# Block kernel on one core: step 10's maximum in attention is issued behind step 9's low half

## The chip, the cores and the metric

The kernel is one program on one core of a Trainium2 chip. The metric is the device time of one execution in microseconds (us), as the median of several runs. All engines of the core run their own instruction streams and wait for each other by semaphores: TensorE (PE, with its weight loads as PEld), VectorE (DVE), ScalarE (ACT), GpSimd (POOL) and SyncE (SP, which issues transfers).

## The reference

One layer of a hybrid block on 512 latent tokens and 256 context tokens, width 2048. One projection of the normed and modulated tokens feeds grouped-query attention (12 query heads of 128, 4 key heads) and a Fourier mixing branch, both gated; the branches are merged by sigmoid gates and projected out. The part that the change touches is the softmax:

```
s = jnp.einsum('bqhgd,bkhd->bhgqk', qi, k, preferred_element_type=jnp.float32)
w = jax.nn.softmax(s, axis=-1).astype(v.dtype)
return jnp.einsum('bhgqk,bkhd->bqhgd', w, v)
```

There are 768 keys: the 512 latent tokens and the 256 context tokens. All products are kept at full float32 precision: each operand is split into a high and a low half, and a product is three matmuls.

## The kernel before

Attention is a loop over i = 0 to 47, twelve heads by four blocks of 128 queries (4 * NH steps), with three more rounds for the tail. In this text "step 10" is i = 10, the eleventh. A step has these parts, which stand in different rounds of the loop:

- `scores(i)`: six matmuls make the 128x768 scores, as 512 and 256 columns in three matmuls each; the DVE takes the negated maximum (TENSOR_REDUCE, L1494), and the ACT the exponential with its row sum (L1496). Below these are the scores, the maximum and the exponential of step i.
- `turn(i)`, one round later: six transposes on PE (L1512) turn the 128x768 probabilities; `split_from` then makes their high half on the ACT (L179, `pth`) and their low half on the DVE (L180, `ptl`). The high and low half of two steps fill one pair of tiles.
- `divide(i)`: the reciprocal of the row sum on the DVE (L1505) and a scaling of the head's gate on the ACT (L1506).
- `values(half)`, for two steps together: eighteen matmuls of 256 columns on PE that read `pth` and `ptl`, two transposes (L1527), then a copy (L1537) and a product (L1538).

Beside this run the filler (`fill`: matmuls of the Fourier branch's projection, with weights `whi` and `wlo` and 512 columns each, for which the DVE multiplies results at L1460), the turning of the next head's queries (L1359) and of the next key group's keys (L1352), sums of weights on POOL, and gate products (L1332). At the end of the loop the first matmuls of the next stage, `a_group(0)`, take the filler's place.

Where the data lies matters for the order. One PSUM tile `banks` of eight banks of 512 columns holds everything. Scores take columns 0 to 767, 768 to 1535 and 1536 to 2303 in turn (`wide[0]` to `wide[2]`), so two neighbours share bank 1; the turned probabilities lie at 2304 to 3071 (`wide[3]`), and share bank 4 with the third. A matmul into a shared bank waits until the other tenant has been read. So step 13's second piece waits for step 11's exponential, the scores of the third place for the low half of a turn, and so on.

The order of the instructions on each engine is not that of the loop. A scheduler lays all engines' streams out from the recorded work; `tc.issue_after(x)` keeps an instruction behind x. Each engine then works through its stream in order, and waits where an operand isn't there. So a change of one place in the order can shift all that follows it in the stage.

Of the kernel before, what the change touches and what calls it, by code (L numbers as in the profile page):

```python
# [27 lines left out]
NKEY = T + C  # L28
# [61 lines left out]
CHUNKS = (0, 2, 1, 3)  # L90
BRANCH_A, BRANCH_B = 10, (6, 7)
A_CHUNKS = ((0, 2), (1, 3))
SUM_AT = (10, 13, 16, 19, 25, 28)
CHAIN_FROM = {BRANCH_A + 1: 3, 8: 2, 9: 2}
HALVED = (8, BRANCH_A + 1)
# [26 lines left out]
def block_kernel(ctx, tc, xT, ctx_rows, ctx_toks, x, c_row, w_ss, w_gate, vecs, qkg, rope, dft_c, dft_s,  # L122
# [55 lines left out]
    def split_from(src, hi, lo):  # L178
        first = nc.scalar.activation(hi, src, ACT.Copy)  # L179
        return first, nc.vector.tensor_tensor(lo, src, hi.bitcast(F32), op=ALU.subtract)  # L180
# [149 lines left out]
    def give(*ts):  # L330
        free.extend(home.pop(id(t))[0] for t in ts)

    def mm3(o, ah, al, bh, bl, start, stop, cont=False):

        nc.tensor.matmul(o, ah, bh, start=start, stop=False, skip_group_check=cont)  # L335
        nc.tensor.matmul(o, ah, bl, start=False, stop=False, skip_group_check=cont)  # L336
        nc.tensor.matmul(o, al, bh, start=False, stop=stop, skip_group_check=cont)  # L337
# [1145 lines left out]
    def scores(i):  # L1483
        h, t = divmod(i, 4)
        kh, kl = kv[h // GQ][:2]
        s = slice(t * P, (t + 1) * P)
        qh, ql = qs[h][:, 0, s], qs[h][:, 1, s]
        sc = next_wide()

        m = 512 if sc is not wide[1] else 256  # L1490
        for a, b in ((0, m), (m, NKEY)):
            mm3(sc[:, a:b], qh, ql, kh[:, a:b], kl[:, a:b], True, True)
        mx = stats[:, 4 * (i % 4) : 4 * (i % 4) + 4]
        maxima[0] = nc.vector.tensor_reduce(mx[:, 0:1], sc[:, :NKEY], axis=AX.X, op=ALU.max, negate=True)  # L1494
        probs[i] = take((NKEY,))
        maxima[1] = nc.scalar.activation(probs[i], sc[:, :NKEY], ACT.Exp, bias=mx[:, 0:1], accum_out=mx[:, 1:2])  # L1496
        if t == 3:
            give(qs.pop(h))

    def divide(i):  # L1500

# [6 lines left out]
    def turn(i):  # L1508
        p = probs.pop(i)
        tp = wide[3]  # L1510
        for k in range(KT):
            nc.tensor.transpose(tp[:, k * P : (k + 1) * P], p[:, k * P : (k + 1) * P], ident)  # L1512
        if i % 2 == 0:
            pts[i // 2] = [atp.tile([P, KT, 256], F32R, tag=n, bufs=2, name=uid(n)) for n in ("pth", "ptl")]
        c = slice((i % 2) * P, (i % 2) * P + P)
        split_from(tp[:, :NKEY].rearrange("p (k q) -> p k q", k=KT), *(w[:, :, c] for w in pts[i // 2]))
        give(p)

    def values(half):
        h, second = divmod(half, 2)  # L1520
# [126 lines left out]
    for i in range(NSTEP + 3):  # L1647
        h, t = divmod(i, 4)
        if i < NSTEP:
            if t == 2 and h + 2 < NH:  # L1650
                load_head(h + 2)
            if i % 12 == 10 and i // 12 + 1 < NKV:
                get_keys(i // 12 + 1)
            scores(i)
        want = min(3 + 61 * (i + 1) // NSTEP, 64) + (i == NSTEP - 1)
        if want > filled:
            fill(1)
            filled += 1
        if i % 2 == 0 and i >= 4:
            values((i - 4) // 2)  # L1660
        if 1 <= i <= NSTEP:
            turn(i - 1)
            divide(i - 1)
        if t == 1 and h + 1 < NH:
            turn_queries(h + 1, b1())
        if want > filled:
            fill(want - filled)
            filled = want
        n = next((n for n, at in enumerate(SUM_AT) if at <= i < at + 3), None)
        if n is not None:  # L1670
            step = i - SUM_AT[n]
            if step == 0:
                weight_sum(n)
            else:
                summed[-1][step]()
            if step == 2:
                give(summed.pop()[0])
        if i == 3:
            with tc.issue_after(maxima[0].ins), tc.issue_after(maxima[1].ins):
                e = take((1024,))  # L1680
                silu_of_row(1, e)
                give(e)
        if i == 33:
            for p in more_raw:
                raw_pools.remove(p)
                retired.append(p)
                if not any(r is p for a in ahead for r, _ in a.raws):
                    free.append(p[0::2])
        if i in GATE_STEPS:
            n = NGATE + GATE_STEPS.index(i)  # L1690
            use_gate(n, get_aside(("gate", n)), maxima[0])
            if n == 2 * KK - 1:
                raw_pools.append((rp, 1, "raw0", 1))
        for q, name in {43: [(0, "Z5"), (0, "S3")], 44: [(0, "S2")], 45: [(0, "S4")], 47: [(1, "Z5")], 48: [(1, "S3")],
                        49: [(1, "S2"), (1, "S4")]}.get(i, ()):
            branch_forms(q, name)
        if i == NSTEP - 1:
            a_groups.append(a_group(0))
            first = a_groups[0].steps("P1")
        if NSTEP > i - 2 >= NSTEP - 3:  # L1700
            next(first)
            next(first)
# [322 lines left out]
```

## Time and profile before

| | |
|---|---|
| median of 3 runs | 1297.37 us (1297.19 to 1297.37) |
| profiled execution, its own time | 1296.21 us |
| span of the profiled execution, first to last instruction | 1294.4 us |
| PE busy / DVE busy / ACT busy | 1277.4 / 996.1 / 683.9 us |
| the attention loop's place in the span | about 815 to 1012 us |
| PE / DVE / ACT busy in these 197 us | 196.10 / 165.75 / 134.38 us |
| granted TensorE clock over the span | 0.995 |

The span leaves 1.81 us of the profiled execution's time outside it. PE is counted as busy until the modelled end of a matmul, which lies later than the start of the next one; a short wait is therefore seen best as the distance between the starts of two instructions that follow each other. In the timeline's rows stand the start in us, the duration in us, the engine, the line, the operation, output and inputs, how many such instructions the row merges, and in brackets the idle time before it with what ended it.

### The profile page before, as it was taken

The page shows a single profiled execution, that of the slowest core. Times are in us where ns is not written, and L with a number is a line of the kernel's source. Part 1 is how long each engine was busy: PE and PEld are TensorE (multiplying, and loading weights), DVE is VectorE, ACT ScalarE, POOL GpSimd, SP SyncE. Part 2 cuts the span into 40 slices and gives each one's busy share as a digit, 9 for nine tenths or more (in the row PEclk, how much of TensorE's full clock was granted, in tenths as well). Part 3 has the DMA queues.
Part 4 walks back from the last instruction along what each step waited for, and adds up shares of the span by engine and source line. Part 5 has one row for each costly group of instructions (what it writes and reads, how often), then busy time and mean ns, then how long its engine had stood idle before and what let it go on. Part 6 is the DMA issues. An engine that isn't in the chain of part 4 may idle for free.

```text
span 1294.4 us, 17701 instructions
## 1 busy us (share of the span) xinstructions
PE 1277.4 (99%) x6598; PEld 1051.3 (81%) x6598; DVE 996.1 (77%) x1304; ACT 683.9 (53%) x1076; POOL 168.8 (13%) x222
## 2 busy tenths in 40 slices
PE   8999999999999999999999999999999999999997
PEld 5677988888888888888888888888888888888885
DVE  5667899979778787658687756788898777887776
ACT  5322655545455454443355544666667646464554
POOL 0000011110102111012021010011100211211210
PEclk8999999999999999999999999999999999999999
DMA  9999588888899889977879897578862899998985
GB/s 378 408 368 352 197 225 215 241 228 262 207 314 244 254 281 289 291 196 188 272 206 277 274 233 254 177 239 253 262 186 74 247 247 256 246 207 237 220 202 171
DMA packets 104487, 319.61 MB, mean 247 GB/s; under 512 B 9904, under 2 KB 33072, under 8 KB 100432
## 3 DMA queue, kind: packets, MB, share of 16 engines
q1 hardware_dynamic: 55056, 197.86, 42.2%
q0 software_dynamic: 27024, 98.19, 35.9%
q10 hardware_dynamic: 22320, 22.42, 5.1%
q8 instruction: 52, 0.85, 0.3%
q14 instruction: 35, 0.29, 0.1%
HBM read 283.82 MB, written 34.61 MB: 246 GB/s over the span
## 4 chain that ended last, share of the span: by engine, by line
PE 93%; DVE 2%; DMA 2%; ACT 2%; issue 1%; SPq 0%; ACTq 0%; DVEq 0%
PE banks L335 11%; PE banks L336 10%; PE banks L337 10%; PE x L335 9%; PE x L337 9%; PE x L336 9%; PE y L336 7%; PE y L335 7%; PE y L337 7%; PE banks L1512 2%; PE pd L563 2%; PE pb L335 2%; PE pb L336 2%; PE pb L337 1%; PE pc L335 1%; PE pc L337 1%
## 5 line engine op out<-in xcount | busy, mean ns | idle before, releaser
L179 ACT ACTIVATE whi<-R 128x1024 fp32r<-128x1024 f32 x138 | 145.4, 1058 | 143.2 <-PE banks L337 47.6
L180 DVE TENSOR_TENSOR wlo<-R,whi 128x1024 fp32r<-128x1024 f32 x138 | 167.5, 1220 | 55.5 <-ACT whi L179 55.3
L180 DVE TENSOR_TENSOR wlo<-wr,whi 128x1024 fp32r<-128x1024 f32 (+1 forms) x122 | 147.1, 1211 | 65.5 <-ACT whi L179 65.4
L179 ACT ACTIVATE whi<-wr 128x1024 fp32r<-128x1024 f32 (+1 forms) x122 | 127.4, 1051 | 126.9 <-PE y L337 41.6
L335 PE MATMUL banks<-whi,s 128*128 128x512 f32 x396 | 157.1, 397 | 1.0 <-DVE ev L1085 1.0
L336 PE MATMUL banks<-wlo,s 128*128 128x512 f32 x396 | 155.2, 392 | 0.0
L337 PE MATMUL banks<-whi,s 128*128 128x512 f32 x396 | 155.0, 391 | 0.0
L335 PE MATMUL x<-whi,s 128*128 128x512 f32 x352 | 137.1, 390 | 0.0
L337 PE MATMUL x<-whi,s 128*128 128x512 f32 x352 | 137.0, 389 | 0.0
L336 PE MATMUL x<-wlo,s 128*128 128x512 f32 x352 | 137.0, 389 | 0.0
L335 PE MATMUL y<-whi,s 128*128 128x512 f32 x316 | 123.0, 389 | 0.6 <-DVE cxe L1235 0.6
L336 PE MATMUL y<-wlo,s 128*128 128x512 f32 x316 | 123.1, 389 | 0.1
L337 PE MATMUL y<-whi,s 128*128 128x512 f32 x316 | 122.8, 389 | 0.0
L288 POOL DMA_DIRECT2D R<-in_w_g x64 | 55.9, 873 | 412.2 <-DVE wlo L180 242.3
L179 ACT ACTIVATE s<-wr 128x512 fp32r<-128x512 f32 (+2 forms) x93 | 60.4, 677 | 70.3 <-DMA wr<-cf_d 23.9
L180 DVE TENSOR_TENSOR s<-wr,s 128x512 fp32r<-128x512 f32 (+2 forms) x93 | 66.8, 747 | 32.9 <-ACT s L179 32.0
L335 PEld LDWEIGHTS banks<-whi,s 128*128 128x128 f32 x396 | 74.4, 188 | 16.8 <-issue 1.4
L337 PEld LDWEIGHTS banks<-whi,s 128*128 128x128 f32 x396 | 74.4, 188 | 15.5
L336 PEld LDWEIGHTS banks<-wlo,s 128*128 128x128 f32 x396 | 74.5, 188 | 14.0 <-DVE wlo L180 0.3
L336 PEld LDWEIGHTS x<-wlo,s 128*128 128x128 f32 x352 | 66.1, 188 | 13.8 <-DVE wlo L180 0.2
L337 PEld LDWEIGHTS x<-whi,s 128*128 128x128 f32 x352 | 66.1, 188 | 13.7
L335 PEld LDWEIGHTS x<-whi,s 128*128 128x128 f32 x352 | 66.1, 188 | 13.6
(321 smaller groups left out, 2826.9 us busy)
## 6 DMA issues: line engine op xcount, KB each, us to landing
wr<-in_w_g SPq DMA_DIRECT2D x128, 512.0 KB, 5.9
R<-in_w_g POOLq DMA_DIRECT2D x64, 512.0 KB, 7.5
wa<-in_w_ss SPq DMA_DIRECT2D x31, 1024.0 KB, 9.5
R<-in_w_g SPq DMA_DIRECT2D x32, 512.0 KB, 5.9
wr<-in_w_gate SPq DMA_DIRECT2D x32, 512.0 KB, 5.2
wr<-in_w_o SPq DMA_DIRECT2D x24, 512.0 KB, 7.2
R<-in_w_o POOLq DMA_DIRECT2D x24, 512.0 KB, 9.5
wr<-in_w_pab SPq DMA_DIRECT2D x20, 512.0 KB, 5.7
```

Of the source, the lines that this page charges most:

```text
L179: first = nc.scalar.activation(hi, src, ACT.Copy)
L180: return first, nc.vector.tensor_tensor(lo, src, hi.bitcast(F32), op=ALU.subtract)
L288: nc.gpsimd.dma_start(chain[e.pc], e.nxt, accum_op=ALU.add)
L335: nc.tensor.matmul(o, ah, bh, start=start, stop=False, skip_group_check=cont)
L336: nc.tensor.matmul(o, ah, bl, start=False, stop=False, skip_group_check=cont)
L337: nc.tensor.matmul(o, al, bh, start=False, stop=stop, skip_group_check=cont)
L563: nc.tensor.matmul(acc[32 * j : 32 * j + 32], c2[:, n, :], w[:, k, :], start=n < 4, stop=n >= KK - 4)
L1512: nc.tensor.transpose(tp[:, k * P : (k + 1) * P], p[:, k * P : (k + 1) * P], ident)
```

## The change

`scores` is cut in two. It keeps the matmuls; the maximum and the exponential move to `weigh(i, sc)`. For every step but step 10, `weigh` is called straight behind `scores`, as before. For step 10 it is called after `turn(9)`, with the maximum and the exponential kept behind the low half that `turn(9)` makes (`split_from` returns both halves, and `turn` now returns the second). `give` of the turned tile and of the query tile change places with lines beside them. No instruction is added or taken away.

```diff
--- before.py
+++ after.py
@@ -90,6 +90,7 @@
 CHUNKS = (0, 2, 1, 3)
 BRANCH_A, BRANCH_B = 10, (6, 7)
 A_CHUNKS = ((0, 2), (1, 3))
+BEHIND = (10,)
 SUM_AT = (10, 13, 16, 19, 25, 28)
 CHAIN_FROM = {BRANCH_A + 1: 3, 8: 2, 9: 2}
 HALVED = (8, BRANCH_A + 1)
@@ -1490,12 +1491,15 @@
         m = 512 if sc is not wide[1] else 256
         for a, b in ((0, m), (m, NKEY)):
             mm3(sc[:, a:b], qh, ql, kh[:, a:b], kl[:, a:b], True, True)
+        if t == 3:
+            give(qs.pop(h))
+        return sc
+
+    def weigh(i, sc):
         mx = stats[:, 4 * (i % 4) : 4 * (i % 4) + 4]
         maxima[0] = nc.vector.tensor_reduce(mx[:, 0:1], sc[:, :NKEY], axis=AX.X, op=ALU.max, negate=True)
         probs[i] = take((NKEY,))
         maxima[1] = nc.scalar.activation(probs[i], sc[:, :NKEY], ACT.Exp, bias=mx[:, 0:1], accum_out=mx[:, 1:2])
-        if t == 3:
-            give(qs.pop(h))
 
     def divide(i):
 
@@ -1513,8 +1517,8 @@
         if i % 2 == 0:
             pts[i // 2] = [atp.tile([P, KT, 256], F32R, tag=n, bufs=2, name=uid(n)) for n in ("pth", "ptl")]
         c = slice((i % 2) * P, (i % 2) * P + P)
-        split_from(tp[:, :NKEY].rearrange("p (k q) -> p k q", k=KT), *(w[:, :, c] for w in pts[i // 2]))
         give(p)
+        return split_from(tp[:, :NKEY].rearrange("p (k q) -> p k q", k=KT), *(w[:, :, c] for w in pts[i // 2]))[1]
 
     def values(half):
         h, second = divmod(half, 2)
@@ -1651,7 +1655,9 @@
                 load_head(h + 2)
             if i % 12 == 10 and i // 12 + 1 < NKV:
                 get_keys(i // 12 + 1)
-            scores(i)
+            sc = scores(i)
+            if i not in BEHIND:
+                weigh(i, sc)
         want = min(3 + 61 * (i + 1) // NSTEP, 64) + (i == NSTEP - 1)
         if want > filled:
             fill(1)
@@ -1659,7 +1665,10 @@
         if i % 2 == 0 and i >= 4:
             values((i - 4) // 2)
         if 1 <= i <= NSTEP:
-            turn(i - 1)
+            split = turn(i - 1)
+            if i in BEHIND:
+                with tc.issue_after(split.ins):
+                    weigh(i, sc)
             divide(i - 1)
         if t == 1 and h + 1 < NH:
             turn_queries(h + 1, b1())
```

The scheduler's order changes from step 10 to the end of the loop on all engines; on POOL and SP a few transfers trade places with neighbours. Line numbers of the changed kernel are higher: L335 to L337 become L336 to L338, L1494 becomes L1500, L1512 becomes L1516.

On the DVE around step 10, before: the first row is the low half of a head's turned queries, then stands step 10's maximum, then the low half of step 7; the two rows of `ptl877_6853` are the low halves of steps 8 and 9, and the second TENSOR_REDUCE is step 11's maximum.

```order
L180 TENSOR_TENSOR s878_6862<-banks_6496,s878_6862 128x512
L1494 TENSOR_REDUCE gain_102<-banks_6496 128x1
L180 TENSOR_TENSOR ptl872_6776<-banks_6496,pth871_6775 128x6x128
L1460 TENSOR_TENSOR R1_1330<-banks_6496,R1_1330 128x512
L180 TENSOR_TENSOR wlo936_7393<-wr896_6972,whi935_7392 128x1024
L180 TENSOR_TENSOR ptl877_6853<-banks_6496,pth876_6852 128x6x128
L1505 RECIPROCAL gain_102<-gain_102 128x1
L180 TENSOR_TENSOR s883_6878<-banks_6496,s882_6877 128x768
L1538 SCALAR_TENSOR_TENSOR s860_6658<-banks_6496,R3_1332 128x256
L1494 TENSOR_REDUCE gain_102<-banks_6496 128x1
L1548 TENSOR_TENSOR s860_6658<-s860_6658 128x2x256
```

After: step 10's maximum follows the second row of `ptl877_6853`, and step 11's maximum stands two rows behind it.

```order
L181 TENSOR_TENSOR s878_6862<-banks_6496,s878_6862 128x512
L181 TENSOR_TENSOR ptl872_6776<-banks_6496,pth871_6775 128x6x128
L1461 TENSOR_TENSOR R1_1330<-banks_6496,R1_1330 128x512
L181 TENSOR_TENSOR wlo936_7393<-wr896_6972,whi935_7392 128x1024
L181 TENSOR_TENSOR ptl877_6853<-banks_6496,pth876_6852 128x6x128
L181 TENSOR_TENSOR s883_6878<-banks_6496,s882_6877 128x768
L1542 SCALAR_TENSOR_TENSOR s860_6658<-banks_6496,R3_1332 128x256
L1552 TENSOR_TENSOR s860_6658<-s860_6658 128x2x256
L181 TENSOR_TENSOR ptl877_6853<-banks_6496,pth876_6852 128x6x128
L1500 TENSOR_REDUCE gain_102<-banks_6496 128x1
L1509 RECIPROCAL gain_102<-gain_102 128x1
L1500 TENSOR_REDUCE gain_102<-banks_6496 128x1
```

The maximum went from ahead of step 7's low half to behind step 9's; the reciprocal between the two maxima is step 10's, and needs step 10's exponential.

On PE after step 13's six transposes, before (the transposes stand just ahead of the first row; `whi887` and `wlo888` are filler weights, `s882` and `s883` the keys' halves, `s904` and `s878` queries): three filler matmuls, six of step 16's scores, two more filler matmuls and one of step 15's second piece, which lies in the bank that the turned probabilities share.

```order
L335 MATMUL banks_6496<-whi887_6887,s837_6467 128x512
L336 MATMUL banks_6496<-wlo888_6888,s837_6467 128x512
L337 MATMUL banks_6496<-whi887_6887,s838_6468 128x512
L335 MATMUL banks_6496<-s882_6877,s904_7055 128x512
L336 MATMUL banks_6496<-s883_6878,s904_7055 128x512
L337 MATMUL banks_6496<-s882_6877,s904_7055 128x512
L335 MATMUL banks_6496<-s882_6877,s904_7055 128x256
L336 MATMUL banks_6496<-s883_6878,s904_7055 128x256
L337 MATMUL banks_6496<-s882_6877,s904_7055 128x256
L335 MATMUL banks_6496<-whi887_6887,s837_6467 128x512
L336 MATMUL banks_6496<-wlo888_6888,s837_6467 128x512
L335 MATMUL banks_6496<-s882_6877,s878_6862 128x256
```

After, with the six transposes as the first row; the last row is the same matmul of step 15.

```order
L1516 MATMUL banks_6496<-ident_86,s901_7033 128x128 x6
L336 MATMUL banks_6496<-s882_6877,s904_7055 128x256
L337 MATMUL banks_6496<-s883_6878,s904_7055 128x256
L338 MATMUL banks_6496<-s882_6877,s904_7055 128x256
L338 MATMUL banks_6496<-whi887_6887,s838_6468 128x512
L336 MATMUL banks_6496<-s882_6877,s904_7055 128x512
L337 MATMUL banks_6496<-s883_6878,s904_7055 128x512
L336 MATMUL banks_6496<-pth902_7045,s885_6883 128x256
L338 MATMUL banks_6496<-s882_6877,s904_7055 128x512
L336 MATMUL banks_6496<-s882_6877,s878_6862 128x256
```

Between the transposes and step 15's second piece stood eight matmuls of 512 columns and three of 256. Now four of 512 and four of 256 stand there: scores of steps 16 and 17, one filler matmul and one of `values(6)`.

On PE at step 45, before (`s1036` is step 45's probabilities, `whi1002` and `wlo1003` the first weights of the next stage): four transposes, nine matmuls of the next stage, the last two transposes, and then three more.

```order
L1512 MATMUL banks_6496<-ident_86,s1036_8401 128x128 x4
L335 MATMUL banks_6496<-whi1002_8016,s861_6661 128x512
L336 MATMUL banks_6496<-wlo1003_8017,s861_6661 128x512
L337 MATMUL banks_6496<-whi1002_8016,s861_6661 128x512
L335 MATMUL banks_6496<-whi1002_8016,s861_6661 128x512
L336 MATMUL banks_6496<-wlo1003_8017,s861_6661 128x512
L337 MATMUL banks_6496<-whi1002_8016,s861_6661 128x512
L335 MATMUL banks_6496<-whi1002_8016,s861_6661 128x512
L336 MATMUL banks_6496<-wlo1003_8017,s861_6661 128x512
L337 MATMUL banks_6496<-whi1002_8016,s861_6661 128x512
L1512 MATMUL banks_6496<-ident_86,s1036_8401 128x128 x2
L335 MATMUL banks_6496<-whi1002_8016,s861_6661 128x512
```

After: the last matmul of step 47's scores and five filler matmuls stand ahead of the two transposes; behind them come one matmul of `values(22)`, the next stage's first three matmuls, and the six transposes of step 46 (`s1040`).

```order
L338 MATMUL banks_6496<-s989_7917,s1026_8259 128x256
L337 MATMUL banks_6496<-wlo995_7928,s837_6467 128x512
L338 MATMUL banks_6496<-whi994_7927,s838_6468 128x512
L336 MATMUL banks_6496<-whi994_7927,s837_6467 128x512
L337 MATMUL banks_6496<-wlo995_7928,s837_6467 128x512
L338 MATMUL banks_6496<-whi994_7927,s838_6468 128x512
L1516 MATMUL banks_6496<-ident_86,s1036_8401 128x128 x2
L336 MATMUL banks_6496<-pth1037_8412,s992_7923 128x256
L336 MATMUL banks_6496<-whi1002_8016,s861_6661 128x512
L337 MATMUL banks_6496<-wlo1003_8017,s861_6661 128x512
L338 MATMUL banks_6496<-whi1002_8016,s861_6661 128x512
L1516 MATMUL banks_6496<-ident_86,s1040_8429 128x128 x6
```

The next stage's first matmul writes bank 0, in which step 47's scores lie until its exponential has read them. Before, the last matmul of step 47's scores stood 30 rows of the order ahead of it; now six matmuls and two transposes stand between them.

## Prediction

> **What bounds the kernel now.** I read the page first, then the stretch of the attention loop, then its waits, and then single rows of the timeline.
>
> ```profile
> span 1294.4 us, 17701 instructions
> PE 1277.4 (99%) x6598; PEld 1051.3 (81%) x6598; DVE 996.1 (77%) x1304; ACT 683.9 (53%) x1076; POOL 168.8 (13%) x222
> ...
> PE 93%; DVE 2%; DMA 2%; ACT 2%; issue 1%; SPq 0%; ACTq 0%; DVEq 0%
> ```
>
> PE sets the end: it is busy 99% of the span and carries 93% of the chain that ended last. The change neither adds nor removes matmuls, so the time can move only by what PE waits. In the attention loop:
>
> ```profile
> core 0: us, PE busy (x) PEld busy (x) DVE busy (x) ACT busy (x) POOL busy (x), PEclk, DMA share, GB/s
> ...
> 815.00:1012.00 197.00, 196.10 (x1308) 172.07 (x1307) 165.75 (x269) 134.38 (x261) 26.86 (x43) 1.00 0.62 189
> ```
>
> ```profile
> PEld banks L1512 <- DVE ptl L180: 2.9, 8, 0.8
> PEld banks L1512 <- ACT s L1496: 1.8, 6, 0.4
> PEld banks L335 <- ACT s L1496: 1.1, 3, 0.7
> ```
>
> The first table shows little idle PE (0.9 us), because a matmul is counted until its modelled end; the second counts the waits at the weight loads (total, times, longest), and the distances between starts, from step 8's transposes (852.04 below, 0.58 late) to the matmul at 1006.32 (0.10 late), give 49 late starts with 5.5 us in all. So a gain is bounded by 5.5 us, a loss isn't bounded by anything here. The DVE is busy 84% of these 197 us: what is queued on it ahead of a low half arrives late.
>
> **Durations.** These rows give the chains between PE instructions.
>
> ```profile
> 848.67 0.87 PE L1512 MATMUL banks<-ident,s 128*128 128x128 f32 x6
> ...
> 851.23 0.39 PE L337 MATMUL banks<-s,s 128*128 128x512 f32 x1
> 852.04 0.87 PE L1512 MATMUL banks<-ident,s 128*128 128x128 f32 x6 [0.42 <-DVE ptl L180]
> ...
> 854.90 0.44 PE L1352 MATMUL banks<-ident,wr 128*128 128x128 f32 x2
> ...
> 857.23 0.44 PE L1512 MATMUL banks<-ident,s 128*128 128x128 f32 x2
> ...
> 868.01 0.82 PE L1512 MATMUL banks<-ident,s 128*128 128x128 f32 x6
> ```
>
> ```profile
> 846.79 0.96 DVE L1494 TENSOR_REDUCE gain<-banks 128x1 f32<-128x768 f32 x1 [0.45 <-PE banks L337]
> ...
> 850.16 0.96 DVE L1494 TENSOR_REDUCE gain<-banks 128x1 f32<-128x768 f32 x1
> 851.04 0.95 DVE L180 TENSOR_TENSOR ptl<-banks,pth 128x768 fp32r<-128x768 f32 x1
> ...
> 853.89 0.96 DVE L180 TENSOR_TENSOR ptl<-banks,pth 128x768 fp32r<-128x768 f32 x1 [0.17 <-ACT pth L179]
> ...
> 859.75 1.21 DVE L1332 SCALAR_TENSOR_TENSOR wr<-wr,crow 128x1024 f32<-128x1024 f32 x1
> 860.89 0.08 DVE L1332 DVE_READ_ACCUMULATOR wr<-wr,crow 128x1 f32 x1
> ```
>
> ```profile
> 847.85 0.90 ACT L1496 ACTIVATE s<-banks,gain 128x768 f32<-128x768 f32 x1 [0.40 <-DVE gain L1494]
> ...
> 849.58 0.81 ACT L179 ACTIVATE pth<-banks 128x768 fp32r<-128x768 f32 x1
> ...
> 853.05 0.81 ACT L179 ACTIVATE pth<-banks 128x768 fp32r<-128x768 f32 x1
> ...
> 857.70 0.81 ACT L179 ACTIVATE pth<-banks 128x768 fp32r<-128x768 f32 x1 [1.25 <-PE banks L1512]
> ```
>
> ```profile
> 846.36 0.39 PE L337 MATMUL banks<-s,s 128*128 128x512 f32 x1
> ...
> 955.53 0.80 ACT L179 ACTIVATE pth<-banks 128x768 fp32r<-128x768 f32 x1
> 956.22 0.89 ACT L1496 ACTIVATE s<-banks,gain 128x768 f32<-128x768 f32 x1
> 957.26 0.39 PE L335 MATMUL banks<-s,s 128*128 128x256 f32 x1 [0.36 <-ACT s L1496]
> ```
>
> Start to start: six transposes to their high half 0.91 (848.67, 849.58); the last two alone 0.47 (857.23, 857.70); high half to low half 0.84 (853.05, 853.89); low half to the PE instruction behind it 1.01 (853.89, 854.90); last matmul of the scores to the maximum 0.43 (846.36, 846.79), and 0.32 where that matmul has 256 columns, whose duration is 0.11 shorter; maximum to exponential 1.06 (846.79, 847.85); exponential to PE 1.04 (956.22, 957.26); high half to the next ACT instruction 0.69 (955.53, 956.22); on a busy DVE one of these maxima or low halves holds the queue 0.88 (850.16, 851.04), a gate product 1.14 (859.75, 860.89). PE's own pace:
>
> ```profile
> 871.76 0.28 PE L336 MATMUL banks<-ptl,s 128*128 128x256 f32 x1
> 871.88 0.28 PE L337 MATMUL banks<-pth,s 128*128 128x256 f32 x1
> ...
> 872.21 0.82 PE L1512 MATMUL banks<-ident,s 128*128 128x128 f32 x6
> 872.79 0.48 PE L335 MATMUL banks<-whi,s 128*128 128x512 f32 x1
> 873.10 0.40 PE L336 MATMUL banks<-wlo,s 128*128 128x512 f32 x1
> 873.34 0.39 PE L337 MATMUL banks<-whi,s 128*128 128x512 f32 x1
> ```
>
> 0.12 for 256 columns, 0.23 for 512, and 0.65 for six transposes (0.89 from 872.21 to 873.10, less one matmul), so 0.11 each.
>
> **The change part by part.** Each term is a place where the order changed: what PE does between two points against the chain that runs beside it.
>
> (1) *Step 10's maximum leaves its old place.* It started at 850.16, and step 7's low half, whose high half was under way at 849.58 and which could have begun at 849.58 + 0.84 = 850.42, began at 851.04. PE, free at 851.23 + 0.23 = 851.46, began step 8's transposes at 852.04. Without the maximum ahead the low half is done 0.62 earlier, and the wait goes: -0.58.
>
> (2) *Steps 10 to 14.* The maximum now follows step 9's low half, so step 10's exponential falls just ahead of step 10's transposes, and step 11's exponential stands behind step 10's high half on the ACT: 0.91 + 0.69 + 1.04 = 2.64 from step 10's transposes until step 13's second piece, in the shared bank, may start. PE has 0.65 + 0.12 + 0.22 + 0.69 + 0.23 = 1.91 between them (six transposes, one matmul of values, two transposes, three scores, one filler): +0.73. Step 13's maximum then waits on the DVE behind step 11's maximum, a gate product, step 10's low half and smaller rows, and step 14's first matmul needs step 13's exponential: by the scores alone it is 0.3 short, with the DVE's queue about 0.9; I take +0.7, nearer the queue, since 0.88 + 1.14 + 0.88 already lie in it. Two small waits add 0.3 (the first product of values(4) with step 9's low half, and step 16's scores behind the turned queries' high half). Before, the same stretch lost 0.6 in six late starts, from 857.23 (0.12 late) to 868.01 (0.09 late). Net +1.1, bounds +0.3 and +1.7.
>
> (3) *Step 15's second piece*, in the turned probabilities' bank, needs step 13's low half. Step 16's maximum stands ahead of that half on the DVE: its last score matmul starts 0.65 + 0.24 = 0.89 behind the transposes' start, the maximum at 1.21, the half at 2.09, and PE is let go at 3.10. PE has 0.65 + 4 x 0.23 + 4 x 0.12 = 2.05: +1.05. With the maximum not in the way it would be 2.76 - 2.05 = +0.7, the lower bound.
>
> (4) *values(10)* has one matmul that reads step 21's high half, only two matmuls of 512 columns behind step 21's transposes: 0.65 + 0.46 = 1.11, where the chain is 0.91 + 0.87 (the high half's 0.81 and 0.06 until PE starts, as from 1005.23 to 1006.10 in the rows of (5)) = 1.78: +0.67. Before, eleven matmuls stood there. Lower bound +0.4, if other waits fall just ahead.
>
> (5) *The loop's end.* Behind the last two transposes of step 45 come one matmul of values(22) and then the next stage's first matmul, which needs bank 0, and so step 47's exponential. That stands on the ACT behind step 45's high half: 0.47 + 0.69 + 1.04 = 2.20. PE has 0.22 + 0.12 = 0.34: +1.86. The two transposes themselves wait for step 46's exponential: 0.32 + 1.06 + 1.04 = 2.42 behind its last score matmul, with 2.06 of PE work between (three matmuls of 256 columns, five transposes, five matmuls of 512): +0.36. Step 46's transposes need step 45's low half at 0.47 + 0.84 + 1.01 = 2.32, and PE comes there later: nothing. Before:
>
> ```profile
> 1005.23 0.81 ACT L179 ACTIVATE pth<-banks 128x768 fp32r<-128x768 f32 x1 [0.22 <-PE banks L1512]
> ...
> 1005.73 0.40 PE L335 MATMUL banks<-whi,s 128*128 128x512 f32 x1
> 1006.10 0.38 PE L335 MATMUL banks<-pth,s 128*128 128x256 f32 x1
> 1006.32 0.39 PE L336 MATMUL banks<-wlo,s 128*128 128x512 f32 x1
> ```
>
> Here the same high half cost 0.14 and a slow start behind it 0.1. Net +2.0; lower bound +1.0, since values(22) alone waits 0.47 + 0.87 - 0.22 = 1.12 for the high half.
>
> (6) *The rest of the loop.* The scheduler laid out all later steps anew. Counted in the same way, each order has some two dozen further places that are short by up to 0.2, and the trace before has a longer wait at 957.26 that came from the ACT's queue. I take 0, and ±1 for what such queues do in the new order. Transfers that changed places with a neighbour on SP and POOL cost nothing so long as PE finds its weights: no wait of PE on a DMA stands among those above.
>
> The sum is -0.58 + 1.1 + 1.05 + 0.67 + 2.0 = +4.2 us. The profiled execution took 1296.21 us, which makes 1300.4; it stands 1.16 us below the median of the runs, 1297.37, and the runs are what is compared, so the forecast is 1301.6 us.
>
> The granted clock is 1.00 in the stretch above, although PE waits there dozens of times. The Trainium skill's page "TensorE: Matmul & The Clock Gate", section "Part 1: The HAM clock gate (the "warmup" mystery)", halves the clock only after an idle window of about 3.4 us; its section "A second HAM failure mode: psum-queue depth-cycling" also has frequent short idles set it swinging. By the first the sum stays, by the second each window at half clock would add about 1.7 us, an estimate from that page's window. The trace agrees with the first up to waits of 0.6 us; a wait of 1.86 it does not show.
>
> **Rivals.** (A) *Not slower: the cover holds.* The only wait that matters is the one removed in (1), and PE finds work elsewhere: 1297.37 - 0.6 = 1296.8. For it: before, most places with short cover lost 0.1 or nothing. Against: a stream is worked in order, and in (5) the work that could cover stands behind the waiting matmul. It decides at (5): the wait at the next stage's first matmul would have to be below 0.6, less than the high half alone. (B) *Half of it*: the queues are kinder, (2) and (6) come out low, 1297.37 + 2 = 1299.4. (C) *Weights arrive late.* Filler matmuls that stood behind step 10's transposes are now ahead, some 2 us earlier:
>
> ```profile
> wr<-in_w_pab SPq DMA_DIRECT2D x20, 512.0 KB, 5.7
> ```
>
> A load takes 5.7 us to land; if two of them come short by the 2 us, that is +4 on top: 1305.6. Against it: PE had no such wait before.
>
> **Numbers.** The forecast (waits as worked out, +2.6 to +6) has 0.67, B 0.15, A 0.07, C and a clock that drops 0.11. The likeliest one's own range is 1300.0 to 1303.4. The range for 8 in 10 is 1298.7 to 1304.4: the lower bounds of the terms add to +1.6 with (1) and (6) at nothing and a little below, the upper ones to +6, and the top reaches into C. 0.2% is 2.6 us, about what a measurement here tells from no change: slower than 1299.96 has 0.76 (C and the forecast without 0.02 at its foot), within 1294.78 and 1299.96 has 0.20 (B, that foot and 0.03 of A), faster 0.04, that part of A in which the later waits of before vanish as well.
>
> **What would show it.** In the profile after: step 8's transposes start without a wait behind step 7's low half; one wait near 1.9 us on PE at the loop's end, released by an exponential (L1502), and one near 0.4 ahead of it by step 46's; a wait near 1 us by a low half (L181) at a score matmul some 14 us behind step 9; waits of 0.7 by exponentials at steps 13 and 14. It would be wrong if the wait at the end is below 1 us, or if PE waits for weights or a transfer in the loop.

## The result and the profile after

| | before | after |
|---|---|---|
| median of six runs each | 1296.98 us | 1304.59 us |
| from, to | 1295.28, 1297.37 | 1302.92, 1307.13 |
| ratio, with its 95% interval | | 1.0055 (1.0043 to 1.0068) |
| profiled execution, its span | 1296.21, 1294.4 us | 1302.92, 1301.1 us |

The changed kernel is slower by 7.6 us. In two more sets of runs, reported below, it had medians of 1303.64 and 1304.85 us, and its seventeen runs reach from 1301.74 to 1307.13. The profiled execution is the shortest of the six.

The page of the changed kernel, its head and its chain, and the loop with the same work as the 197 us shown of before (it ends 6.5 us later):

```profile
span 1301.1 us, 17713 instructions
PE 1279.4 (98%) x6598; PEld 1051.7 (81%) x6598; DVE 997.1 (77%) x1304; ACT 684.8 (53%) x1076; POOL 168.7 (13%) x222
...
PE 94%; DVE 2%; DMA 2%; ACT 1%; issue 1%; SPq 0%; ACTq 0%; DVEq 0%
```

```profile
815.00:1018.50 203.50, 198.15 (x1308) 172.08 (x1308) 168.35 (x274) 136.93 (x264) 27.37 (x44) 1.00 0.61 185
```

```profile
PE banks L1516 <- ACT s L1502: 1.9, 3, 1.4
PE banks L336 <- ACT s L1502: 1.4, 3, 0.6
PE banks L336 <- ACT pth L180: 1.3, 2, 0.9
PE banks L336 <- DVE ptl L181: 0.8, 1, 0.8
```

The number of matmuls is the same (x1308) at the full clock (1.00). PE is idle in 5.35 of these us, 0.9 before, and now by waits long enough to show at the matmuls themselves, not only at the weight loads: on exponentials (L1502), high halves (L180) and one low half (L181). The single rows, of the timeline of PE:

```profile
851.71 0.39 PE L338 MATMUL banks<-s,s 128*128 128x512 f32 x1
851.94 0.63 PE L1516 MATMUL banks<-ident,s 128*128 128x128 f32 x4
...
864.36 0.39 PE L336 MATMUL banks<-s,s 128*128 128x256 f32 x1 [0.57 <-ACT s L1502]
867.20 0.39 PE L336 MATMUL banks<-s,s 128*128 128x256 f32 x1 [0.30 <-ACT s L1502]
878.08 0.39 PE L336 MATMUL banks<-s,s 128*128 128x256 f32 x1 [0.75 <-DVE ptl L181]
908.64 0.39 PE L336 MATMUL banks<-pth,s 128*128 128x256 f32 x1 [0.43 <-ACT pth L180]
914.53 0.44 PE L1516 MATMUL banks<-ident,s 128*128 128x128 f32 x2 [1.35 <-ACT s L1502]
959.90 0.33 PE L1516 MATMUL banks<-ident,s 128*128 128x128 f32 x1 [0.39 <-ACT s L1502]
1007.69 0.44 PE L1516 MATMUL banks<-ident,s 128*128 128x128 f32 x2 [0.15 <-ACT s L1502]
1009.02 0.38 PE L336 MATMUL banks<-pth,s 128*128 128x256 f32 x1 [0.90 <-ACT pth L180]
1009.91 0.50 PE L336 MATMUL banks<-whi,s 128*128 128x512 f32 x1 [0.50 <-ACT s L1502]
```

The first two rows are step 8's transposes, which now start 0.23 behind the matmul ahead of them: no wait. The others are late starts, in order of time: step 13's second piece, step 14's first matmul, step 15's second piece, values(10), two transposes of step 22, a transpose of step 33, two of step 45, values(22), and the next stage's first matmul. As in the prediction, a late start is the distance from the start ahead less PE's own pace (0.12, 0.23 or 0.11). Added up by place, those over 0.045 us (row (2) begins at 854.90 us of before, so it has 0.83 where the prediction counted 0.6 from 857.23 on):

| place | before | after | difference | forecast |
|---|---|---|---|---|
| (1) step 8's transposes | 0.63 | 0.00 | -0.63 | -0.58 |
| (2) steps 10 to 14 | 0.83 | 1.84 | +1.01 | +1.1 |
| (3) step 15's second piece | 0.00 | 1.13 | +1.13 | +1.05 |
| (4) values(10) | 0.21 | 0.72 | +0.51 | +0.67 |
| (5) the loop's end | 0.25 | 2.36 | +2.11 | +2.0 |
| step 22's transposes | 0.06 | 1.62 | +1.56 | in (6) |
| all other places | 4.09 | 4.52 | +0.43 | (6): 0 |

The sum is +6.1, from 6.1 to 12.2 us. With 1.0 at the stage's first filler matmuls, which both have, it is 7.1 and 13.2; the sums of late starts below include it. Another 0.4 lies ahead of the loop and 0.2 in late starts too small for the table, and from the next stage to the end the two executions run 6.69 us apart without a change. The medians differ by 7.6 us; the other 0.9 is not in this pair of executions.

**Step 22** is the place that was not foreseen. Its chain, in rows of DVE, SP, ACT and PE, before:

```profile
898.54 1.23 DVE L180 TENSOR_TENSOR wlo<-wr,whi 128x1024 fp32r<-128x1024 f32 x1
899.68 0.95 DVE L1494 TENSOR_REDUCE gain<-banks 128x1 f32<-128x768 f32 x1
...
899.79 0.33 SPq L215 DMA_DIRECT2D wr<-in_w_pab  x1
...
903.99 1.06 ACT L179 ACTIVATE whi<-wr 128x1024 fp32r<-128x1024 f32 x1 [0.94 <-DMA wr<-in_w_pab]
```

and after:

```profile
901.56 0.95 DVE L1500 TENSOR_REDUCE gain<-banks 128x1 f32<-128x768 f32 x1
902.43 1.22 DVE L1333 SCALAR_TENSOR_TENSOR wr<-wr,crow 128x1024 f32<-128x1024 f32 x1
...
903.57 0.95 DVE L181 TENSOR_TENSOR s<-banks,s 128x768 fp32r<-128x768 f32 x1
904.44 1.22 DVE L181 TENSOR_TENSOR wlo<-wr,whi 128x1024 fp32r<-128x1024 f32 x1
...
905.68 0.33 SPq L216 DMA_DIRECT2D wr<-in_w_pab  x1
...
911.37 1.06 ACT L180 ACTIVATE whi<-wr 128x1024 fp32r<-128x1024 f32 x1 [1.61 <-DMA wr<-in_w_pab]
...
912.62 0.88 ACT L1502 ACTIVATE s<-banks,gain 128x768 f32<-128x768 f32 x1
...
913.50 0.89 ACT L1502 ACTIVATE s<-banks,gain 128x768 f32<-128x768 f32 x1
```

A weight's low half (`wlo`) is the last reader of a load buffer. It stood ahead of step 21's maximum on the DVE; now that maximum, a gate product and a split of the keys stand ahead of it, so it comes 5.9 us later by the clock (904.44 for 898.54), some 4.0 of them against step 21's maximum, which itself is 1.9 later (901.56 for 899.68). SP can ask for the next weight only then (905.68, right behind 904.44 + 1.22), the weight lands by 911.37, and its high half, which waits 1.61 for it, stands on the ACT ahead of the exponentials of steps 24 and 23. The second of these frees the bank into which step 22's last two transposes go (914.53, 1.35). PE takes the weight itself only at 960.88, with the filler's thirteenth result. Before, the high half waited 0.94 for its load as well, but nothing behind it was short. The load also took longer: 5.69 us from its issue to the start of the high half (905.68, 911.37), 4.20 before (899.79, 903.99).

### The profile page after: what moved, and what is told of

Read it like the earlier page. It is cut to its first block, busy times and chain, and to the rows that moved or that the text cites. A ratio compares the mean times of both kernels' runs of the same rounds, so it can differ in the third digit from the quotient of the medians.

```text
span 1301.1 us, 17713 instructions
## 1 busy us (share of the span) xinstructions
PE 1279.4 (98%) x6598; PEld 1051.7 (81%) x6598; DVE 997.1 (77%) x1304; ACT 684.8 (53%) x1076; POOL 168.7 (13%) x222
## 4 chain that ended last, share of the span: by engine, by line
PE 94%; DVE 2%; DMA 2%; ACT 1%; issue 1%; SPq 0%; ACTq 0%; DVEq 0%
PE banks L336 11%; PE banks L337 10%; PE banks L338 10%; PE x L338 9%; PE x L337 9%; PE x L336 9%; PE y L337 7%; PE y L338 7%; PE y L336 7%; PE banks L1516 2%; PE pd L564 2%; PE pb L336 1%; PE pb L337 1%; PE pb L338 1%; PE pc L336 1%; PE pc L338 1%
## 5 line engine op out<-in xcount | busy, mean ns | idle before, releaser
L180 ACT ACTIVATE whi<-R 128x1024 fp32r<-128x1024 f32 x138 | 145.3, 1058 | 144.2 <-PE banks L338 48.5
L181 DVE TENSOR_TENSOR wlo<-R,whi 128x1024 fp32r<-128x1024 f32 x138 | 167.6, 1221 | 55.4 <-ACT whi L180 55.2
L181 DVE TENSOR_TENSOR wlo<-wr,whi 128x1024 fp32r<-128x1024 f32 (+1 forms) x122 | 147.3, 1213 | 69.2 <-ACT whi L180 69.0
L180 ACT ACTIVATE whi<-wr 128x1024 fp32r<-128x1024 f32 (+1 forms) x122 | 127.6, 1051 | 129.3 <-PE y L338 42.3
L336 PE MATMUL banks<-whi,s 128*128 128x512 f32 x396 | 157.2, 397 | 1.5 <-DVE ev L1086 1.0
L338 PE MATMUL banks<-whi,s 128*128 128x512 f32 x396 | 155.4, 392 | 0.0
L337 PE MATMUL banks<-wlo,s 128*128 128x512 f32 x396 | 155.1, 392 | 0.0
L336 PE MATMUL x<-whi,s 128*128 128x512 f32 x352 | 137.3, 390 | 0.0
L338 PE MATMUL x<-whi,s 128*128 128x512 f32 x352 | 137.1, 390 | 0.0
L337 PE MATMUL x<-wlo,s 128*128 128x512 f32 x352 | 137.1, 389 | 0.0
L337 PE MATMUL y<-wlo,s 128*128 128x512 f32 x316 | 123.2, 390 | 0.7 <-DVE wlo L181 0.7
L336 PE MATMUL y<-whi,s 128*128 128x512 f32 x316 | 123.1, 389 | 0.0
L338 PE MATMUL y<-whi,s 128*128 128x512 f32 x316 | 122.9, 390 | 0.0
L180 ACT ACTIVATE s<-wr 128x512 fp32r<-128x512 f32 (+2 forms) x93 | 60.4, 677 | 70.9 <-DMA wr<-cf_d 24.1
L181 DVE TENSOR_TENSOR s<-wr,s 128x512 fp32r<-128x512 f32 (+2 forms) x93 | 66.9, 749 | 32.4 <-ACT s L180 31.4
L336 PEld LDWEIGHTS banks<-whi,s 128*128 128x128 f32 x396 | 74.5, 188 | 17.5 <-issue 1.4
L338 PEld LDWEIGHTS banks<-whi,s 128*128 128x128 f32 x396 | 74.4, 188 | 15.5
L337 PEld LDWEIGHTS banks<-wlo,s 128*128 128x128 f32 x396 | 74.5, 188 | 14.0 <-DVE wlo L181 0.2
L337 PEld LDWEIGHTS x<-wlo,s 128*128 128x128 f32 x352 | 66.1, 188 | 13.8
L338 PEld LDWEIGHTS x<-whi,s 128*128 128x128 f32 x352 | 66.1, 188 | 13.6
L336 PEld LDWEIGHTS x<-whi,s 128*128 128x128 f32 x352 | 66.1, 188 | 13.6
```

## Experiments

The theory tested is that of places: the loss is the sum of PE's waits where the new order leaves too little work as cover. Rival 1: a late maximum costs by itself. Rival 2: any order but the tuned one costs. Each time below is a median; the ratio behind it is to the kernel before, run beside it in the same set, with the 95% interval in brackets. The medians of before were 1297.37 us in the set of after_again, behind7, whi_behind and end_early, 1297.15 in that of after_third, load_small, step_47 and steps_4_29, and 1296.56 in that of gs_late and steps_4_29_gs.

**after_again, after_third.** The changed kernel, unchanged.

> The changed kernel once more, beside the others on one chip. The theory of places (the time lost is the sum of PE's waits at the places where the new order leaves too little work as cover): 1304.6 us, with the late starts of the attention loop adding to about 13.2 us as against 7.1 before, and the largest ones at step 22's last transposes (1.5), at the next stage's first matmul with the product of values(22) ahead of it (1.8), at step 15's second piece (0.9), step 13's second piece (0.7), values(10) (0.6), step 33's transposes (0.5) and step 14's scores (0.5). The rival (the loss comes from the late maximum itself) expects the same time.

> The changed kernel a third time, as the reference on this chip: 1304 us. If the wait at step 22's transposes hangs on the landing of a weight load, it differs from run to run (it was 1.51 and 1.13 so far), while the waits at steps 13 to 15, at values(10) and at the loop's end repeat to 0.02 us.

1303.64 us, 1.0041 (1.0029 to 1.0054), and 1304.85 us, 1.0061 (1.0049 to 1.0073). Steps 13, 14, 15 and values(10) repeat within 0.01 (0.73, 0.47, 0.92, 0.60), and so do step 45, values(22) and the next stage's first matmul (0.31, 1.06, 0.77). Step 22 was 1.51, 1.13 and 1.23 late, and from the load's issue to the start of the high half it took 5.69, 5.31 and 5.42 us: the wait is what this time has over 4.2 us, so it hangs on a transfer. In the third set one thing came on top, at the loop's end:

```profile
1007.85 0.44 PE L1516 MATMUL banks<-ident,s 128*128 128x128 f32 x2
1009.19 0.39 PE L336 MATMUL banks<-pth,s 128*128 128x256 f32 x1 [0.90 <-ACT pth L180]
1010.08 0.78 PE L336 MATMUL banks<-whi,s 128*128 128x512 f32 x1 [0.50 <-ACT s L1502]
1010.65 0.63 PE L337 MATMUL banks<-wlo,s 128*128 128x512 f32 x1
...
1013.60 0.40 PE L338 MATMUL banks<-whi,s 128*128 128x512 f32 x1
```

```profile
1010.00:1011.00 1.00, 0.92 (x2) 0.82 (x3) 1.00 (x4) 1.00 (x3) 0.00 (x0) 0.56 0.52 57
1011.00:1012.00 1.00, 1.00 (x5) 0.71 (x4) 1.00 (x2) 0.78 (x2) 0.00 (x0) 0.50 0.31 29
1012.00:1013.00 1.00, 1.00 (x6) 1.00 (x5) 0.53 (x1) 0.00 (x0) 0.17 (x1) 0.50 0.36 29
1013.00:1014.00 1.00, 1.00 (x4) 0.80 (x4) 0.13 (x1) 0.97 (x2) 0.71 (x1) 0.73 0.20 20
```

Here the granted clock falls to 0.50 for some 3.4 us behind the two waits, and matmuls of 512 columns take 0.63 in place of 0.40. The late starts from 1000 us on add to 4.17 us, against 2.62 and 2.61 in the two profiled executions in which the clock held.

**behind7.** Step 10's maximum two rows behind its old place: step 7's low half and a filler product now stand ahead of it.

```diff
...
             split = turn(i - 1)
+            splits[i - 1] = split
+            old = splits.get(i - 3)
             if i in BEHIND:
-                with tc.issue_after(split.ins):
+                with tc.issue_after(old.ins):
```

> Step 10's maximum is still asked for behind a low half of turned probabilities, but that of step 7, one row further down the DVE's queue than before, and not that of step 9. Theory of places: step 8's transposes lose their wait of 0.58, a wait of about 0.7 by a low half or an exponential appears near step 20, and from step 22 on the order is that of before: 1296.6 us, between 1295.9 and 1297.3. Rival 1, a maximum that is asked for later costs by itself, because its scores hold their bank longer: slower than before by a good part of the 7.6 us, at least 1299. Rival 2, every other order than the tuned one costs: at least 1299 as well.

1297.11 us, 0.9997 (0.9988 to 1.0005). The DVE around step 10:

```profile
850.50 0.96 DVE L181 TENSOR_TENSOR ptl<-banks,pth 128x768 fp32r<-128x768 f32 x1 [0.38 <-ACT pth L180]
851.38 0.68 DVE L1461 TENSOR_TENSOR R<-banks,R 128x512 f32<-128x512 f32 x1
851.97 0.95 DVE L1500 TENSOR_REDUCE gain<-banks 128x1 f32<-128x768 f32 x1
```

Step 7's low half begins at 850.50, as (1) had it (850.42), and step 8's transposes start on time; 0.69 comes back at step 20's scores, and the sum of late starts is 7.04, against 7.09 before. Rival 2 falls, since the loop is in another order from step 8 to step 21 at no cost. Rival 1 falls for a maximum that is 1.8 us later than before (851.97 for 850.16); in the changed kernel it is 9.05 us later (859.21).

**whi_behind.** The changed kernel, with the weight's high half kept behind step 23's exponential.

```diff
         maxima[1] = nc.scalar.activation(probs[i], sc[:, :NKEY], ACT.Exp, bias=mx[:, 0:1], accum_out=mx[:, 1:2])
+        exps[i] = maxima[1].ins
...
             with ExitStack() as line:
+                if e.key == ("pab", 3, 6):
+                    line.enter_context(tc.issue_after(exps[23]))
```

> The changed kernel, with one more rule: the high half of the filler's weight whose load lands late stands on the ACT behind step 23's exponential, no longer ahead of step 24's. From step 24 on the order falls back into that of before. Theory of places: the late starts from step 22 on fall from 7.1 us to before's 2.6, since the 1.5 at step 22's transposes, the 0.5 at step 33's and the 2.1 at the loop's end go and before's 0.5 at step 36 comes back; steps 10 to 21 keep theirs: 1304.6 - 4.4 = 1300.2 us, bounds 1299.2 and 1301.2. Rival 1 (the late maximum itself): nothing changes at step 10, so 1304.6. Rival 2 (any other order costs): 1304.6 or more.

1300.00 us, 1.0020 (1.0011 to 1.0028), 3.6 below the changed kernel of the same set. Late starts: 9.47 against 13.34. Steps 13 to 15 and values(10) are as they were (0.74, 0.47, 0.92, 0.60); step 22 falls to 0.15, and the loop's end to 0.25, because behind step 23 the scheduler finds its old order again. What is left over before, 2.6 us, is the price of terms (1) to (4), forecast as +2.24. Step 10's maximum is as late here as in the changed kernel, so no more than these 2.6 us can be put down to its lateness, and the waits at the places account for 2.4 of them (9.47 less 7.09).

**load_small.** No instruction of PE, DVE, ACT or SP changes place; one load is made short.

```diff
+            if e.key == ("pab", 3, 6):
+                asked[0] = asks[0].dma_start(raw[:, :64], src[:, :64])
+                nc.gpsimd.memset(raw[:, 64:], 0.01)
+            else:
                 asked[0] = asks[0].dma_start(raw if len(src.shape) == 2 else raw.rearrange("p (i j c) -> p i j c", i=4, j=2), src)
```

> The changed kernel with its order, but the weight load in question brings 64 of its 1024 columns; the others are set on the POOL, so one of the filler's weights is left out for fifteen sixteenths. No instruction of PE, DVE, ACT or SP changes its place. If step 22's wait comes from that load's landing, through the ACT's queue (the high half of the weight stands ahead of steps 24's and 23's exponentials), it falls to about 0.15 us: 1304.0 - 1.1 = 1302.9 us, bounds 1302.3 and 1303.4, and the runs scatter less. If the wait comes from the maxima or the scores themselves, it stays at 0.8 to 1.5 and the time at 1304.

```profile
910.65 0.40 ACT L1514 ACTIVATE s<-s,gain 128x128 f32<-128x128 f32 x1
910.94 1.05 ACT L180 ACTIVATE whi<-wr 128x1024 fp32r<-128x1024 f32 x1
```

The high half no longer waits (0.29 behind the scaling ahead of it), and step 22 is 0.15 late. So the wait of step 22 comes from that load. The time is 1303.54 us, 1.0047 (1.0034 to 1.0059): 1.3 below the 1304.85 of the same set, 0.14 above the upper bound, and not clear of the noise, since the two intervals overlap; it is the row of step 22 that shows the cause. The runs reach over 2.4 us and not 3.8. What the load waits for is read from the rows above, not tested apart.

**end_early.** Step 47's scores, maximum and exponential ahead of step 46's values.

```diff
...
-            sc = scores(i)
-            if i not in BEHIND:
+            sc = early.pop(i) if i in early else scores(i)
+            if i not in BEHIND and i != NSTEP - 1:
                 weigh(i, sc)
+            if i == NSTEP - 2:
+                early[i + 1] = scores(i + 1)
+                weigh(i + 1, early[i + 1])
```

> The changed kernel, but step 47's scores, maximum and exponential are written ahead of step 46's values and transposes, so that the exponential which frees the next stage's bank stands ahead of step 45's high half on the ACT. All else in the loop is as in the changed kernel. Theory of places: the 0.31, 1.06 and 0.77 at the loop's end (2.1 us) go, and 0.2 to 1.0 come in their place at step 46's scores and at the first matmul of the next stage: 1304.6 - 1.5 = 1303.1 us, bounds 1302.4 and 1303.7. Both rivals: 1304.6, since step 10 is where it was.

1301.45 us, 1.0026 (1.0017 to 1.0035): 2.2 below the changed kernel, more than the bounds allowed. Late starts from 1000 us on fall from 2.61 to 1.03, the 1.5 that was expected; the largest is 0.49 at the next stage's first matmul. Step 22 is 0.8 late in this profiled execution and not 1.1, again with a shorter load (5.01 us from 905.34 to the high half at 910.35). That the rest is a clock that no longer drops is possible, but no profiled execution of this set shows it.

**steps_4_29 and step_47.** The same change elsewhere: `BEHIND = (4, 29)` and `BEHIND = (47,)`.

> The same change at steps 4 and 29 and not at step 10: each of these maxima is asked for behind the low half of the step ahead. Theory of places: in the order that results, the 0.58 at step 8's transposes and the 0.52 at step 36's scores go, and a handful of places with about 0.2 come; counted by the chains of the prediction the loop is 1.6 us better than before's: 1295.8 us, bounds 1294.9 and 1296.7, so faster than both. Rival 1 (a late maximum costs by itself, as step 10's did): 1300 or more, twice over. Rival 2 (any other order than the tuned one costs): 1299 or more.

> The same change at the loop's last step alone, so that nothing ahead of step 45 moves. Theory of places: waits of 2.4 at step 45's last transposes, 1.1 at values(22), 0.9 at step 46's transposes and 2.0 at the next stage's first matmul, which now needs an exponential behind step 46's low half, with only 0.2 of that stretch there before: 1297.4 + 6.2 = 1303.6 us, bounds 1302.4 and 1304.8. Rival 2 (any other order costs, by how much of the order is other): only some fifty instructions change their place, against several hundred for step 10, so 1299 at most.

step_47: 1304.86 us, 1.0064 (1.0051 to 1.0077), at the upper bound. The waits stand where they were expected: 2.31 at step 45's last transposes, 1.06 at values(22), 0.88 at step 46's transposes, 1.67 at the next stage's first matmul. The clock is at 0.50 from 1010 to 1015 us. Some fifty instructions in another place cost as much as several hundred.

steps_4_29: 1303.06 us, 1.0049 (1.0036 to 1.0062), where 1295.8 was expected. The loop did become better, with late starts of 6.06, 1.0 below before's. The time went behind the loop:

```profile
PE banks L1630 <- DMA s<-yb_d: 4.1, 1, 4.1
...
R<-in_w_pab POOLq DMA_DIRECT2D x5, 512.0 KB, 13.2
...
s<-yb_d POOLq DMA_DIRECT2D x1, 512.0 KB, 18.8
```

These are PE's only wait behind 1020 us, and the transfers of 1020 to 1050 us with their time from issue to landing; before, no such wait, and for the same transfers:

```profile
R<-in_w_pab POOLq DMA_DIRECT2D x6, 512.0 KB, 7.7
...
s<-yb_d POOLq DMA_DIRECT2D x1, 512.0 KB, 11.0
```

The two orders differ on POOL in one thing that reaches here: the gate's small transfer (`gs` from `gcol`, which is turned while it is written) was issued at 997.4 us before, and at 1012.3 us now, behind two loads of the next stage.

**gs_late.** The kernel before, with that one transfer moved; the order of everything else is that of before.

```diff
...
-    nc.gpsimd.dma_start(gs.rearrange("k p -> p k"), gcol)
...
-        nc.gpsimd.dma_start(ga[half, j], g_d[0, half, j].rearrange("p (t c) -> p t c", t=2))
+        load = nc.gpsimd.dma_start(ga[half, j], g_d[0, half, j].rearrange("p (t c) -> p t c", t=2))
+        if len(ga) == 2 and not asked_gs:
+            with tc.issue_after(load.ins):
+                asked_gs.append(nc.gpsimd.dma_start(gs.rearrange("k p -> p k"), gcol))
```

> The kernel before, with one transfer moved on the POOL's queue and nothing else: the gate's small one (gs from gcol, which took 12.3 us to land) is asked for behind the second load of the next stage's gates, some 15 us later, as the order of the steps 4 and 29 had it by itself. If that place is what held the branch's transposes there (4.1 us, a transfer of yb_d that landed 18.8 us after its issue instead of 11.0), PE waits some 4 us at the branch's first transposes: 1297.2 + 4 = 1301 us, and 1303 with a clock that drops in the wait; bounds 1300 and 1304. If the wait came from the loop's end being reached about 1 us earlier, the time stays at 1297.2.

1304.36 us, 1.0054 (1.0042 to 1.0067), 0.4 above the upper bound: one transfer of the gate's 16 columns costs as much as the whole change. Rows of PE, then the core's windows at the same place, of this kernel:

```profile
1047.79 1.97 PE L1629 MATMUL banks<-ident,s 128*128 128x128 f32 x8 [5.49 <-DMA s<-yb_d]
1049.41 0.78 PE L335 MATMUL banks<-whi,s 128*128 128x512 f32 x1
```

```profile
1012.00:1024.00 12.00, 12.00 (x64) 10.29 (x63) 10.64 (x17) 8.92 (x14) 3.45 (x5) 1.00 0.63 95
...
1045.00:1050.00 5.00, 2.21 (x10) 2.11 (x11) 1.23 (x1) 0.09 (x1) 0.86 (x1) 0.50 1.06 274
```

and of before:

```profile
1000.00:1005.00 5.00, 5.00 (x36) 4.49 (x34) 4.64 (x10) 4.64 (x9) 1.76 (x3) 1.00 0.10 4
1005.00:1010.00 5.00, 5.00 (x32) 4.13 (x31) 4.60 (x8) 3.75 (x7) 1.10 (x2) 1.00 0.37 30
...
1012.00:1024.00 12.00, 12.00 (x64) 10.31 (x63) 10.63 (x17) 8.92 (x14) 2.40 (x5) 1.00 1.03 355
```

While the small transfer is under way (12.5 us from issue to landing) the core moves 95 GB/s, not 355; what was asked for behind it lands late, PE waits 5.5 us, and the clock falls to 0.50. The kernel before shows the same at the old place, where the transfer is under way from 997.4 to 1009.7 us: in the first two of its rows the core moves 4 and 30 GB/s, against 96 and 261 in the same stretches of gs_late. No wait of PE followed from that. SP's transfers are held up as well as POOL's: in gs_late the two weight loads that SP asks for between 1016 and 1019 us take 14.5 us to land, 6.9 before.

**steps_4_29_gs.** Steps 4 and 29, with the gate's transfer where it was.

```diff
...
+        if i == 46:
+            nc.vector.tensor_tensor(gcol, gparts[:, :KK], gparts[:, KK:], op=ALU.add)
+            nc.vector.tensor_tensor(gcol, gcol, bada[:, 2 * KK :], op=ALU.add)
+            nc.gpsimd.dma_start(gs.rearrange("k p -> p k"), gcol)
...
```

> Steps 4 and 29 once more, with the gate's small transfer back in its place on the POOL's queue (its two sums on the DVE and the transfer are written into step 46). The loop keeps the 1.0 us that its late starts had less than before's (6.1 against 7.1), and the wait of 4.1 us in the next stage goes: 1297.2 - 1.0 = 1296.2 us, bounds 1295.6 and 1297.0, faster than before by little. If moving the maxima itself had cost the time, it stays at 1303.

1295.77 us against 1296.56, 0.9991 (0.9983 to 1.0000): late starts of 6.14, no wait behind the loop. It is the fastest of all, by an amount at the edge of what the runs can tell. The move that cost 7 us at step 10 costs nothing at steps 4 and 29. It is the same edit, but not the same delay: step 4's maximum starts 3.5 us later by the clock than before (834.39 for 830.92), step 10's 9.05.

## Why the prediction was right, and where not

Slower was right, and so was the mechanism: PE's waits at places named ahead.

- (1) to (5) came within 0.16 us each, together +4.13 against +4.24. The method carries that far: start to start from rows of before, the chain beside PE's own pace. In (2) there is luck as well: step 14's wait was 0.47 where 0.7 was taken, and the small waits of the stretch came to 0.64 where 0.3 was taken. One sum of the prediction does not come out: the lower bounds as printed add to +2.4 with (1) and (6) at nothing, or +1.8 with (1) at -0.58, not to +1.6. Nothing hangs on it, since the time came at the other end.
- Step (6) failed, in the sentence "Transfers that changed places with a neighbour on SP and POOL cost nothing so long as PE finds its weights". PE did find its weight, and yet it paid 1.56 us, because the split that waits for the load stands in the ACT's queue ahead of exponentials. What moved was not SP's order alone, but the place on the DVE of the split that frees the load's buffer; the gate load now ahead of the weight's was itself issued in time. That took the slack away, and the wait is then what the load takes over 4.2 us (5.69 us and 1.51, 5.42 and 1.23, 5.31 and 1.13, 5.01 and 0.82). Why it takes longer than the 4.20 of before was not tested. load_small shows the load's part. gs_late shows for POOL that one transfer in another place, there behind five others, can cost 7 to 8 us.
- The rest of (6), forecast as 0 ± 1, measured +0.43; step 33's 0.5 took the place of step 36's 0.5.
- Rival C had "a clock that drops" at 0.11 with the late weights. Both happened in part. One load came late. The clock dropped in the third profiled execution of this kernel and in that of load_small, each time at the loop's end, and in the third cost about 1.6 us (4.17 less 2.6). So the centre, 1301.6, was 3 us low and the top of the range, 1304.4, 0.2: 1.6 of it by step 22, then the 0.4 ahead of the loop and the 0.4 elsewhere. What remains could be the clock in some of the runs; the profiled one of these six shows no drop in the loop. Rival A fell at (5), where it said that it would be decided: the wait there is 1.83 by two starts, not below 0.6.
- The paragraph on the clock set the Trainium skill's page "TensorE: Matmul & The Clock Gate" against waits of up to 0.6 us. Its section "Part 1: The HAM clock gate (the "warmup" mystery)" asks for an idle window of about 3.4 us before the clock halves. Here 0.50 followed waits of 1.06 and 0.77 with work between them, in two of four profiled executions with the same waits; the half clock then lasted some 3.4 us. That fits the length of the window that the Trainium skill gives, and its remark that the window runs freely, but not a reading by which it must be idle throughout. The measurement decides: waits of about 2 us within 3.4 (0.31, 1.06 and 0.77) were enough, sometimes.

## What to carry to other kernels

When a stream is laid out anew, count not only the chains that PE waits on, but, for each transfer, what frees its buffer, where that instruction went in its own queue, and what stands behind the first reader of the landed data: an in-order queue hands a late load on to work that never needed it. Before calling a small move good or bad, compare places; the same edit cost 7 us at step 10 and at step 47, and nothing at steps 4 and 29, by where the scheduler put a few instructions and one transfer. And look behind the stage: the loss of steps_4_29 lay some 30 us behind the loop that was changed.

## What had not been expected of the hardware

- A transfer of 8 KB that is turned while written took 10.5 to 13.1 us to land in the five traces read for it, and the core's other transfers were held up meanwhile (95 GB/s in place of 355 in 12 us, and 4 and 30 in place of 96 and 261 at its old place). Moved by 15 us it cost 7.8 us of time (1304.36 against 1296.56). It isn't POOL's queue alone that is taken up, since SP's loads landed late too (14.5 us for 6.9); what it is, these runs don't settle.
- The granted clock fell to 0.50 behind waits of only 1.06 and 0.77 us, and not in each execution; behind waits of 4.1 and 5.5 us on a transfer it fell as well. A wait of PE has a price beyond its length.
